# Router and gather on the raw residual sum, the first tile's routing inside the last projection, the expert's activation and down product bank by bank

## The chip, the core and the metric

The kernel runs on one core of one Trainium2 chip. It computes with TensorE (PE, matrix products; its weight loads are PEld), VectorE (DVE), ScalarE (ACT) and GpSimd (POOL); SyncE (SP) does little but issue DMA transfers, in the order of its queue, and an entry that waits holds back all behind it. The metric is the device time of one execution in microseconds (us). Runs of the kernel before lie between 2548.65 and 2553.27 us.

## The reference, cut to what matters

Two kinds of transformer blocks follow each other on 256 tokens of width 1024, all in float32. The change touches the end of the second: a mixer with three branches, gated, merged and projected (`w_out`), and then a mixture of 32 experts of which each token uses 4.

```python
h = rms_norm_2(x, norm_mix[layer]) * (1.0 + sc_m) + sh_m
branches = jnp.stack([o_lru, o_diff, o_swa], axis=2)
branch_proj = jnp.einsum('bsnc,ncd->bsnd', branches, w_branch)
gates = jax.nn.sigmoid(gl).reshape(B, S, N_BRANCHES, D)
merged = jnp.einsum('bsnd,bsnd->bsd', gates, branch_proj)
x = x + g_m * (merged @ w_out)
h = rms_norm_2(x, norm_ffn[layer]) * (1.0 + sc_f) + sh_f
logits = xt @ w_router + b_router            # xt = h
top_v, top_e = lax.top_k(logits, TOP_K)
hcat = x_pad[tok] @ w1[e] + b1[e]
x_glu = jnp.minimum(hcat[:, ::2], SWIGLU_LIMIT)
x_lin = jnp.clip(hcat[:, 1::2], -SWIGLU_LIMIT, SWIGLU_LIMIT)
act = x_glu * jax.nn.sigmoid(SWIGLU_ALPHA * x_glu) * (x_lin + 1.0)
return act @ w2[e] + b2[e]
```

## The kernel before, in words

Weights of the dense products come as 512 KB pieces into four rotating buffers named `raw` (`nraw` is 4); ACT rounds a piece to `whi`, DVE or POOL takes the rest into `wlo`, and PE multiplies three times (L205 to L207). A piece's buffer is free for the next load when both have read it. The kernel is written as a program whose instructions a scheduler puts in order on each engine; a buffer of a pool is handed out in program order, and an instruction that is "pinned" keeps its program order on its engine.

The end of the second block's mixer is written in this order: the sliding-window attention (`swa`, L1127 to L1185, called SWA here: scores L1158, bias L1165, softmax L438 to L453, products L1179 and L1182, and transposes, L233, at its end), then `prepare` (it opens the memory that SWA used as scratch for the experts, loads and prepares the router's constants in `route_prep`, and issues the first `npre` expert units), then `merge` (for each of three branches and two column halves 24 matmuls of a branch projection and 48 of its gate), then the last projection (`gemm` with `w_out`, eight pieces, the first tile of 128 tokens before the second). At the end of a tile its residual sum is formed (`done`), normalised and modulated (`rms_mod`, L872 and L873) and transposed; `route` computes logits, the choice and each token's place, and `moe_gather` collects the rows of a pair of experts by a one-hot product (L1369). The two vectors of the modulation occupy a buffer `AS` until then.

The experts (`moe`, L1535) go in 16 pairs; a pair's weights are 24 units of 1 MB (tiles `mraw`, one of the ring is `AS`), 16 for the up product (L1417) and 8 for the down product (L1456). SP issues all of them (L1482, the last in pieces at L1487) into a ring of 18 slots, each as soon as its slot is free. The first `npre` units go out in `prepare`, the others of the first 18 when the merge and the projection give memory back.

Of the kernel before, what the change touches and what calls it, by code (L numbers as in the profile page):

```python
# [18 lines left out]
P = 128  # L19
# [52 lines left out]
class Kernel:  # L72
    def __init__(self, tc, a, out, dbg=None):
# [7 lines left out]
        self.pre, self.npre = [], 4  # L81
# [32 lines left out]

    def small(self, n, tag="sm", dt=F32):
# [4 lines left out]
    def rsqrt(self, v, eps, n, scale=1.0):  # L120
# [6 lines left out]
        y = self.small(n, "ry")  # L127
# [723 lines left out]
    def rms_mod(self, t, h, A, sh, split=True):  # L851

# [9 lines left out]
        self.normed = nc.vector.tensor_tensor(ss[:, 2:3], ss[:, 0:1], ss[:, 1:2], op=OP.add)  # L862
        r = self.rsqrt(ss[:, 2:3], 1e-6, 1, 1.0 / D)
        xT = self.new_xT(t)
        def part(v, c):

            return v[:, c * 512:c * 512 + 512] if split else v.rearrange("t (p k) -> t k p", k=KD)[:, 4 * c:4 * c + 4]

        for c in range(2):
            s = slice(c * 512, c * 512 + 512)  # L870
            hv = h[:, s] if split else h[:, s].rearrange("t (k p) -> t k p", k=4)
            nc.vector.scalar_tensor_tensor(hv, part(x, c), r[:, 0:1], part(A, c), op0=OP.mult, op1=OP.mult)  # L872
            nc.vector.tensor_tensor(hv, hv, part(sh, c), op=OP.add)  # L873
# [317 lines left out]
    def hybrid_in(self, ctx, gp, first):  # L1191
# [3 lines left out]
        with tc.tile_pool(name="mix2", bufs=1, reuse_waits="tile") as mp:  # L1195
            gm = self.st(gp, [P, D], "gm")
            self.mod_row(gm, 2)
            A, sh = self.mod_pair(self.mods, 3, a["norm_ffn_2"][0])
# [39 lines left out]
            def prepare():  # L1238
# [5 lines left out]
                units(self.npre)  # L1244
# [518 lines left out]
```

## Time and profile before

| | |
|---|---|
| median of 3 runs | 2551.11 us (2548.65 to 2553.27) |
| the profiled execution | 2552.11 us, its span 2550.5 us (1.6 us lie outside the span) |
| PE busy | 2385.5 us, 94% |
| DVE, ACT, POOL busy | 50%, 32%, 9% |
| moved by DMA | 707.49 MB, 277 GB/s on average, 421 GB/s from some 1615 us to 2520 us |
| mean granted clock of TensorE | 0.977 of full speed |

Busy shares are averages over stages with different limits: PE counts as busy in the experts' stage too, where it mostly waits for the weights within a stream that the DMA engines run without a pause. What a stage is worth is read from the windows and from the chain of waits.

### The profile page before, as it was taken

To read this page: it belongs to the slowest core of one execution; us is meant where nothing else is said; L and a number is where in the kernel's file an instruction comes from. 1 tells how busy PE (TensorE), PEld (TensorE's weight loads), DVE (VectorE), ACT (ScalarE), POOL (GpSimd) and SP (SyncE) were. 2 spreads that over 40 slices of the span, in tenths; PEclk is the share of its full clock that TensorE was granted. 3 is DMA by queue.
4 is the path that set the end of the run, shared out by engine and by line. 5 is a ranking of instruction groups with operands and counts; after the bars stand their busy time and mean duration, and the time that the engine had idled before them with its cause. 6 is when DMAs were issued, how large, how long until landed. Compare 5 with 4: busy or idle time off the path is not lost.

```text
span 2550.5 us, 29146 instructions
## 1 busy us (share of the span) xinstructions
PE 2385.5 (94%) x11076; PEld 1571.2 (62%) x11076; DVE 1279.3 (50%) x2126; ACT 817.6 (32%) x1161; POOL 227.1 (9%) x200
## 2 busy tenths in 40 slices
PE   7998999999799999989988988999889998999998
PEld 6887787778678878878867766433333333333332
DVE  6768757576666675675566756222222222222222
ACT  5443544444344454444435653100000010000000
POOL 4000211200200011230022101000000000000000
PEclk9999999999899999999999999999999999999999
DMA  8777465577667656665646367899999999999997
GB/s 267 243 235 232 145 185 181 181 224 226 195 197 234 193 151 185 189 197 175 182 153 214 109 215 265 364 421 421 421 421 421 421 421 421 421 421 421 421 421 285
DMA packets 203145, 707.49 MB, mean 277 GB/s; under 512 B 18090, under 2 KB 31610, under 8 KB 154360
## 3 DMA queue, kind: packets, MB, share of 16 engines
q1 hardware_dynamic: 195368, 684.02, 73.7%
q0 software_dynamic: 7632, 21.55, 2.8%
q8 instruction: 89, 1.46, 0.2%
q14 instruction: 56, 0.46, 0.1%
HBM read 704.39 MB, written 3.47 MB: 278 GB/s over the span
## 4 chain that ended last, share of the span: by engine, by line
PE 40%; DMA 36%; DVE 7%; issue 2%; ACT 2%; POOL 1%; SPq 0%; DVEq 0%; ACTq 0%; POOLq 0%
DMA mraw<-in_w_dram 28%; PE mm L206 10%; PE mm L207 10%; PE mm L205 10%; DMA AS<-in_w_dram 3%; PE mm L1417 3%; PE tp L233 2%; DVE wlo L147 2%; DMA raw<-in_w_in_dram 1%; PE sc L1456 1%; DMA araw<-in_w_ada_dram 1%; ACT whi L143 1%; POOL wlo L147 1%; PE sc L1369 1%; DVE x L274 0%
## 5 line engine op out<-in xcount | busy, mean ns | idle before, releaser
L147 DVE TENSOR_TENSOR wlo<-raw,whi 128x1024 fp32r<-128x1024 f32 (+1 forms) x459 | 568.1, 1244 | 304.4 <-ACT whi L143 302.0
L143 ACT ACTIVATE whi<-raw 128x1024 fp32r<-128x1024 f32 x486 | 509.8, 1055 | 546.9 <-PE mm L207 385.5
L205 PE MATMUL mm<-whi,xTh 128*128 128x512 f32 (+2 forms) x1552 | 598.4, 387 | 9.1 <-ACT whi L143 9.1
L206 PE MATMUL mm<-wlo,xTh 128*128 128x512 f32 (+2 forms) x1552 | 593.0, 383 | 13.0 <-POOL wlo L147 8.9
L207 PE MATMUL mm<-whi,xTl 128*128 128x512 f32 (+2 forms) x1552 | 592.6, 382 | 0.4 <-DVE xTl L147 0.4
L1417 PE MATMUL mm<-mraw,xe 128*64 128x512 f32 x1968 | 495.4, 615 | 49.3 <-DMA mraw<-in_w_dram 49.3
L1417 PEld LDWEIGHTS mm<-mraw,xe 128*64 128x64 f32 x1968 | 156.3, 141 | 367.2 <-issue 265.5
L206 PEld LDWEIGHTS mm<-wlo,xTh 128*128 128x128 f32 x1552 | 294.9, 190 | 73.9 <-POOL wlo L147 11.9
L205 PEld LDWEIGHTS mm<-whi,xTh 128*128 128x128 f32 x1552 | 294.8, 190 | 66.2 <-ACT whi L143 11.7
L207 PEld LDWEIGHTS mm<-whi,xTl 128*128 128x128 f32 x1552 | 294.8, 190 | 52.0 <-DVE xTl L147 1.0
L1426 ACT ACTIVATE mt<-mg 128x256 f32<-128x256 f32 x64 | 26.7, 417 | 812.4 <-DVE mg L1425 762.4
L1425 DVE TENSOR_SCALAR mg<-mm 128x256 f32<-128x256 f32 x64 | 27.2, 425 | 462.1 <-PE mm L1417 457.7
L1456 PE MATMUL sc<-mraw,xTl 128*64 128x512 f32 x936 | 223.4, 594 | 0.2 <-ACT xTl L1440 0.2
L1456 PEld LDWEIGHTS sc<-mraw,xTl 128*64 128x64 f32 x936 | 71.5, 137 | 140.2 <-issue 136.7
L207 PE MATMUL mm<-whi,hl 128*128 128x512 f32 x352 | 138.3, 393 | 0.0
L205 PE MATMUL mm<-whi,hh 128*128 128x512 f32 x352 | 138.1, 392 | 0.0
L206 PE MATMUL mm<-wlo,hh 128*128 128x512 f32 x352 | 138.0, 392 | 0.0
L1461 DVE TENSOR_TENSOR xTh<-sc,gf 128x512 f32<-128x512 f32 x32 | 22.1, 692 | 215.7 <-PE sc L1456 215.7
L822 DVE SCALAR_TENSOR_TENSOR acc<-araw,cond,acc 128x512 f32<-128x512 f32 x96 | 71.8, 748 | 52.5 <-DMA araw<-in_w_ada_dram 51.9
L147 POOL TENSOR_TENSOR wlo<-raw,whi 128x1024 fp32r<-128x1024 f32 x27 | 69.0, 2569 | 281.3 <-ACT whi L143 277.7
L694 POOL TENSOR_TENSOR pj<-pj,gt 128x512 f32<-128x512 f32 x32 | 59.1, 1861 | 193.2 <-DVE gt L693 192.6
L206 PEld LDWEIGHTS mm<-wlo,hh 128*128 128x128 f32 x352 | 66.7, 189 | 13.7
(416 smaller groups left out, 2144.4 us busy)
## 6 DMA issues: line engine op xcount, KB each, us to landing
mraw<-in_w_dram SPq DMA_DIRECT2D x362, 1024.0 KB, 19.8
raw<-in_ffn_up_dram SPq DMA_DIRECT2D x176, 512.0 KB, 4.5
raw<-in_w_in_dram SPq DMA_DIRECT2D x142, 512.0 KB, 4.4
raw<-in_ffn_down_dram SPq DMA_DIRECT2D x88, 512.0 KB, 4.3
araw<-in_w_ada_dram SPq DMA_DIRECT2D x96, 256.0 KB, 4.1
AS<-in_w_dram SPq DMA_DIRECT2D x21, 1024.0 KB, 19.8
raw<-in_w_branch_dram SPq DMA_DIRECT2D x28, 512.0 KB, 3.7
raw<-in_w_out_dram SPq DMA_DIRECT2D x24, 512.0 KB, 4.4
```

What stands on the lines that cost most here:

```text
L143: ins = self.nc.scalar.activation(hi, src, AF.Copy)
L147: ins = (self.nc.gpsimd if pool else self.nc.vector).tensor_tensor(lo, src, hi, op=OP.subtract)
L205: nc.tensor.matmul(banks[b], xh, hi[:, s], start=kc == 0, stop=False)
L206: nc.tensor.matmul(banks[b], xh, lo[:, s], start=False, stop=False)
L207: nc.tensor.matmul(banks[b], xl, hi[:, s], start=False, stop=kc == nk - 1)
L233: self.nc.tensor.transpose(pt[:s.shape[-1], i * P:i * P + s.shape[0]], s, self.ident)
L694: nc.gpsimd.tensor_tensor(m, m, th, op=OP.add)
L822: nc.vector.scalar_tensor_tensor(acc, raw, self.cond[:, k:k + 1], acc, op0=OP.mult, op1=OP.add)
L1417: self.pe(nc.tensor.matmul(ph[nb][e * 64:e * 64 + 64], xe[:, k, e * 64:e * 64 + 64], units[e][k][:, nb * 512:nb * 512 + 512], start=False, ...
L1425: nc.vector.tensor_scalar(g, pv[:, :, 0], 7.0, None, op0=OP.min)
L1426: nc.scalar.activation(th, g, AF.Tanh, scale=0.851)
L1456: self.pe(nc.tensor.matmul(py[c][e * 64:e * 64 + 64], aT[:, k * P + e * 64:k * P + e * 64 + 64], w, start=k == 0, stop=k == 7))
```

## The change

The router and the gather work on the residual sum itself, not on its normalised and modulated copy. The scale per column (`acol`) goes into the router's matrix and, after the gather, into eight small operations per pair; the shift (`scol`) into the router's bias and the same eight; the token's norm (`rn`) multiplies logits and the one-hot matrix. So the two vectors of the modulation are loaded as columns, the buffer `AS` becomes the first slot of the ring (`npre` 5, the ring still has 18), and `route_prep` gains a product of router and shift, `prod`, which takes a buffer of the pool `raw`. The last projection is written out by hand (`out_and_route`, in an order that is kept), with the first tile's routing in it. Softmax and overflow count come behind the first up product (`route_rest`). A pair's activation, transposes and down product go bank by bank (`moe_body`). Every unit is a contiguous megabyte of W1 or W2 now, and the last two units come in halves of columns.

```diff
-        self.pre, self.npre = [], 4
+        self.pre, self.npre = [], 5
...
 
             self.st(mp, [33, 12], "rel")
...
+                units(self.npre - 1)
                 self.mi = 0
                 for src in self.sources(0)[:self.npre]:
...
+            grans = self.load_split(KD, a["w_out_2"][0], 0, D)
+            with self.ordered():
+                self.out_and_route(self.lhs_x(mT), grans, gm)
...
+    def out_and_route(self, lhs, grans, gm):
+
+
+
+
+        nc = self.nc
+        banks = self.banks(D)
+        for t in range(2):
+            self.products(lhs, KD, D, banks[t], t, grans[:1])
+        self.products(lhs, KD, D, banks[0], 0, grans[1:])
+        self.residual(0, 0, banks[0][0], gm)
+        self.residual(0, 1, banks[0][1], gm)
+        self.part(lhs, 1, banks[1][0], 0, grans[1:])
+        self.residual(1, 0, banks[1][0], gm)
+        self.turn(0, 0)
+        self.turn(0, 1)
+        self.part(lhs, 1, banks[1][1], 1, grans[1:4])
+        self.logits(0, 0)
+        self.logits(0, 1)
+        self.choose(0)
+        self.part(lhs, 1, banks[1][1], 1, grans[4:6])
+        self.place(0)
+        self.part(lhs, 1, banks[1][1], 1, grans[6:])
+        self.turn(1, 0)
+        self.gather_begin()
+        self.residual(1, 1, banks[1][1], gm)
+        self.logits(1, 0)
+        self.turn(1, 1)
+        self.logits(1, 1)
+        self.choose(1)
+        self.place(1)
...
+    def mod_cols(self):
...
+        def row(i):
+            return bass.AP(tensor=m.tensor, offset=m.offset + i * D, ap=[[1, P], [P, KD]])
+
+        self.acol, self.scol = col(row(4)), col(row(3))
+        norm = col(a["norm_ffn_2"][0].rearrange("(k p) -> p k", p=P))
+        nc.gpsimd.tensor_tensor(self.acol, self.acol, norm, op=OP.mult)
+        self.wr = self.cp.tile([P, KD, NE], F32, name="wr")
+        nc.gpsimd.dma_start(self.wr, a["w_router_2"][0].rearrange("(k p) n -> p k n", p=P))
...
+        prod = self.st(self.wp, [P, 1024], "raw", bufs=self.nraw)[:, :KD * NE]
+        v = prod.rearrange("p (n k) -> p k n", k=KD)
+        self.pin(nc.vector.tensor_tensor(v, self.wr, self.scol[:, :, None].to_broadcast([P, KD, NE]), op=OP.mult))
+        sw = self.st(mp, [P, NE], "lg0")
+        self.pin(nc.vector.tensor_reduce(sw, prod.rearrange("p (n k) -> p n k", k=KD), axis=AX.X, op=OP.add))
+        self.pin(nc.vector.tensor_tensor(self.wr, self.wr, self.acol[:, :, None].to_broadcast([P, KD, NE]), op=OP.mult))
+        pb = self.ps("tp")[:, :NE]
+        nc.tensor.matmul(pb, one, sw, start=True, stop=True)
+        self.pin(nc.vector.tensor_tensor(br, br, pb, op=OP.add))
...
+    def residual(self, t, h, bank, gm):
+
+        nc = self.nc
+        s = slice(h * 512, h * 512 + 512)
+        ss = self.sx[t]
+        y = self.st(self.fp, [P, 512], "y5", bufs=2)
+        nc.vector.scalar_tensor_tensor(y, bank, 0.5, gm[:, s], op0=OP.mult, op1=OP.mult)
+        nc.vector.tensor_tensor(self.h2[t][:, s], self.x[t][:, s], y, op=OP.add)
+        nc.scalar.activation(y, self.h2[t][:, s], AF.Square, accum_out=ss[:, h:h + 1])
+        if h == 0:
+            nc.vector.tensor_scalar(ss[:, 2:3], ss[:, 0:1], 1.0 / D, 1e-6, op0=OP.mult, op1=OP.add)
+        else:
+            self.rsqrt(ss[:, 1:2], ss[:, 2:3], 1, 1.0 / D, out=self.rn[:, t:t + 1])
+
...
+        lg = self.lg[t]
+        nc.vector.scalar_tensor_tensor(lg, self.pr[:, t * NE:t * NE + NE], self.rn[:, t:t + 1], self.rc[0], op0=OP.mult,
+                                       op1=OP.add)
...
+    def one_hot(self, S, t, pos, w):
+
+        for e in range(2):
+            f = w[:, t:t + 1] if len(w.shape) == 2 else w[:, t, e:e + 1]
+            self.nc.vector.tensor_scalar(S[:, t, e], self.slot, pos[:, t, e:e + 1], f, op0=OP.is_equal, op1=OP.mult)
...
+    def gather_end(self, mp, pg):
+
+        xe = self.st(mp, [P, KD, P], "xe")
+        for c in range(KD):
+            a, b = self.acol[:, c:c + 1], self.scol[:, c:c + 1]
+            src = pg[c // 4][:, c % 4 * P:c % 4 * P + P]
+            if c % 2:
+                self.nc.scalar.activation(xe[:, c], src, AF.Identity, scale=a, bias=b)
+            else:
+                self.nc.vector.tensor_scalar(xe[:, c], src, a, b, op0=OP.mult, op1=OP.add)
...
+    def moe_body(self, mp, ph, act, aT, ys, units, end=None):
+
+        py = [self.ps("sc") for _ in range(2)]
         for nb in range(4):
...
+            self.moe_act(mp, act, ph[nb], nb)
+        self.moe_aT(act, aT, 0)
+        for nb in range(1, 4):
+            self.moe_aT(act, aT, nb)
+            self.moe_down(py, aT, units, nb - 1)
+        if end:
+            end(None)
+        for c in range(2):
+            if end or c == 0:
+                self.moe_down(py, aT, units, 3, (c,) if end else (0, 1), bool(end))
+            self.moe_scale(ys, py, c)
+            if end:
+                end(c)
...
+        def of(w, d):
+            return w[e + d] if isinstance(e, int) else w[bass.ds(e[d], 1)].rearrange("o f n -> (o f) n")
+
+        up = [of(W1, d).rearrange("(k p) n -> p k n", p=P)[:, k] for k in range(KD) for d in range(2)]
+        return up + [of(W2, d).rearrange("(j p r) n -> p j (r n)", p=P, r=2)[:, j] for j in range(4) for d in range(2)]
...
-        ph, xe = self.ph0, self.moe_gather(mp, self.pos[:, :, 0:2])
+        u1, u2 = self.moe_load(0)
+        with self.ordered():
+            self.one_hot(self.S0, 1, self.pos[:, :, 0:2], self.rn)
+            self.gather_tile(self.pg0, self.S0, 1)
+            xe = self.gather_end(mp, self.pg0)
+            ph = self.moe_bias(self.sel, self.b1[0])
+            self.moe_up(xe, ph, u1)
+            self.route_rest(self.bp)
+            for t in range(2):
+                nc.scalar.activation(self.x[t], self.h2[t], AF.Copy)
...
+                self.moe_up(xe, ph, u1)
+            if not end:
+                xe = self.moe_gather(mp, self.pos[:, :, e + 2:e + 4])
+                nxt = self.moe_load(e + 2)
```

On **SP** the program's order around the end of SWA was, before, as follows (`raw` from `w_branch` and `w_in` are pieces for the merge, `mraw` are expert units; 16 pieces for the merge stand ahead of the units, of which the last four are shown):

```order
L219 DMA raw_12746<-in_w_branch_dram 128x2x512
L219 DMA raw_12752<-in_w_branch_dram 128x2x512
L219 DMA raw_12788<-in_w_in_dram 128x2x512
L219 DMA raw_12794<-in_w_in_dram 128x2x512
L1482 DMA mraw_12502<-in_w_2_dram 128x2048
L1482 DMA mraw_12504<-in_w_2_dram 128x2048
L1482 DMA mraw_12506<-in_w_2_dram 128x2048
L1482 DMA mraw_12508<-in_w_2_dram 128x2048
L219 DMA raw_12800<-in_w_in_dram 128x2x512
L219 DMA raw_12806<-in_w_in_dram 128x2x512
```

After the change the same queue reads as follows, from the last two pieces of the gates that stand before SWA's end in both on:

```order
L237 DMA raw_12397<-in_w_in_dram 128x2x512
L237 DMA raw_12403<-in_w_in_dram 128x2x512
L1612 DMA mraw_12528<-in_w_2_dram 128x2048
L1612 DMA mraw_12530<-in_w_2_dram 128x2048
L1612 DMA mraw_12532<-in_w_2_dram 128x2048
L1612 DMA mraw_12534<-in_w_2_dram 128x2048
L237 DMA raw_12536<-in_w_branch_dram 128x2x512
L237 DMA raw_12542<-in_w_branch_dram 128x2x512
L237 DMA raw_12576<-in_w_in_dram 128x2x512
L237 DMA raw_12582<-in_w_in_dram 128x2x512
```

The four units, which wait for SWA's memory, stand ahead of all 28 pieces that the merge still needs; before, they stood ahead of 12 of them.

On **PE** the merge's matmuls (`mm` from `whi` or `wlo`) stood between SWA's before; this is a stretch of them near SWA's end (`tp` with `ident` are transposes, `sc` SWA's products):

```order
L206 MATMUL mm_12693<-wlo_12683,xTh_2403_11114 128x512
L233 MATMUL tp_12275<-ident,s_2650_12236 128x128 x2
L207 MATMUL mm_12693<-whi_12682,xTl_2404_11115 128x512
L205 MATMUL mm_12692<-whi_12688,xTh_2381_10996 128x512
L233 MATMUL tp_12275<-ident,s_2650_12236 128x128 x2
L206 MATMUL mm_12692<-wlo_12689,xTh_2381_10996 128x512
L1179 MATMUL sc_12263<-pj_11990,s_2660_12269 128x64 x4
L233 MATMUL tp_12287<-ident,s_2623_12121 128x128 x4
L207 MATMUL mm_12692<-whi_12688,xTl_2382_10997 128x512
L205 MATMUL mm_12692<-whi_12688,xTh_2381_10996 128x512
L1179 MATMUL sc_12263<-pj_11990,s_2662_12280 128x64 x4
```

After the change SWA's own stand alone, and the first of the branch product follows the last of SWA and the new router product (L1361):

```order
L1184 MATMUL sc_12266<-pj_11993,s_2661_12272 128x64 x4
L251 MATMUL tp_12290<-ident,s_2624_12124 128x128
L1184 MATMUL sc_12266<-pj_11993,s_2663_12283 128x64 x4
L251 MATMUL tp_12290<-ident,s_2624_12124 128x128 x3
L251 MATMUL tp_12297<-ident,s_2624_12124 128x128 x4
L1361 MATMUL tp_12494<-lg_2709_12491,one_12487 128x32
L223 MATMUL mm_12548<-whi_12538,yT1h_2418_11161 128x512
L223 MATMUL mm_12549<-whi_12538,yT1h_2420_11163 128x512
```

Counted over the stretch, 141 of these matmuls stood ahead of SWA's last transposes, and none does now: all 336 (six halves of branch products with 24 each, four halves of gates with 48) follow.

On **DVE**, after the change, SWA's last rows are followed by the preparation of the router, and the first `wlo` of the merge comes some rows behind it:

```order
L471 RECIPROCAL rs_2658_12264<-se_2656_12255 128x4
L1187 TENSOR_TENSOR s_2624_12124<-sc_12266,rs_2658_12264 128x256
L1349 MEMSET tri_12484 128x128
L165 TENSOR_TENSOR yT2l_2423_11166<-tp_12290,yT2h_2422_11165 128x512
L165 TENSOR_TENSOR yT2l_2425_11168<-tp_12297,yT2h_2424_11167 128x512
L1344 TENSOR_TENSOR b_2702_12471<-raw_12470,b_2702_12471 64x512
L1344 TENSOR_TENSOR b_2704_12477<-raw_12476,b_2704_12477 64x512
L1347 TENSOR_TENSOR pick_12482<-ident 128x64
L1353 MEMSET one_12487 128x128
L1356 TENSOR_TENSOR raw_12489<-wr,mc_11147 128x8x32
L1367 MEMSET on_12499 128x32
L1528 CAST sel_12512<-pick_12482 128x512
```

Before, SWA's last group (from one L1182 to the scores' maximum L438 and on) stood on DVE with the pieces' `wlo` between:

```order
L1182 TENSOR_TENSOR s_2623_12121<-sc_12212,rs_2644_12210 128x256
L147 TENSOR_TENSOR wlo_12683<-raw_12680,whi_12682 128x1024
L1165 SCALAR_TENSOR_TENSOR s_2650_12236<-sc_12237,ry_2615_12084,s_2607_12065 128x256
L1165 SCALAR_TENSOR_TENSOR s_2650_12236<-sc_12238,ry_2615_12084,s_2607_12065 128x256
L1165 SCALAR_TENSOR_TENSOR s_2650_12236<-sc_12237,ry_2615_12084,s_2607_12065 128x256
L1165 SCALAR_TENSOR_TENSOR s_2650_12236<-sc_12238,ry_2615_12084,s_2607_12065 128x256
L147 TENSOR_TENSOR wlo_12689<-raw_12686,whi_12688 128x1024
L438 TENSOR_REDUCE mx_2653_12247<-s_2650_12236 128x4
L440 TENSOR_TENSOR mx_2653_12247<-mx_2653_12247,sk_2603_12055 128x4
L442 TENSOR_SCALAR nb_2654_12250<-mx_2653_12247 128x4
```

In the rows of after no `wlo` stands before SWA's end; `raw` at L1356 is `prod`, and the pieces of the merge that come later in the program get their `raw` buffers behind it.

At the end of the last projection PE's order is now this, from the projection's last matmul to the first up product (`tp` with `h` transposes, `sc` from `S` and `h` is the gather, `mm` from `wr` the logits):

```order
L1308 MATMUL mm_13200<-whi_13193,xTl_2849_13099 128x512
L251 MATMUL tp_13362<-ident,h_13145 128x128 x4
L1480 MATMUL sc_13368<-S_2906_13370,h_13144 128x128 x4
L1480 MATMUL sc_13369<-S_2906_13370,h_13144 128x128 x4
L1406 MATMUL mm_13327<-wr,xTh_2901_13360 128x32 x4
L251 MATMUL tp_13403<-ident,h_13145 128x128 x4
L1406 MATMUL mm_13327<-wr,xTh_2901_13360 128x32 x4
L1430 MATMUL mm_13327<-mask_12504,tri_12484 128x32
L1432 MATMUL mm_13327<-mask_12504,one_12487 128x32
L1480 MATMUL sc_13368<-S_2906_13370,h_13145 128x128 x4
L1480 MATMUL sc_13369<-S_2906_13370,h_13145 128x128 x4
L1535 MATMUL mm_13518<-b_2702_12471,sel_12512 128x512
```

Of the gather of the first pair the first tile's half stands ahead of the second tile's choice, and no operation on `h` as a whole stands between the residual sum and the transposes.

## Rows read from the trace of the kernel before

**Rows 1.** The page: bytes in 40 equal slices, the chain by line, one DMA line.

```profile
GB/s 267 243 235 232 145 185 181 181 224 226 195 197 234 193 151 185 189 197 175 182 153 214 109 215 265 364 421 421 421 421 421 421 421 421 421 421 421 421 421 285
...
DMA mraw<-in_w_dram 28%; PE mm L206 10%; PE mm L207 10%; PE mm L205 10%; DMA AS<-in_w_dram 3%; PE mm L1417 3%; PE tp L233 2%; DVE wlo L147 2%; DMA raw<-in_w_in_dram 1%; PE sc L1456 1%; DMA araw<-in_w_ada_dram 1%; ACT whi L143 1%; POOL wlo L147 1%; PE sc L1369 1%; DVE x L274 0%
...
raw<-in_w_in_dram SPq DMA_DIRECT2D x142, 512.0 KB, 4.4
```

**Rows 2.** Windows by stage (from:to, length, busy time by engine, clock, DMA share, GB/s).

```profile
1457.40:1504.00 46.60, 44.42 (x243) 35.31 (x243) 32.24 (x67) 25.89 (x59) 1.19 (x3) 1.00 0.47 142
...
1522.00:1557.40 35.40, 34.78 (x143) 27.86 (x144) 26.40 (x23) 20.28 (x22) 7.05 (x4) 0.94 0.80 264
...
1586.20:1609.30 23.10, 15.37 (x89) 14.27 (x87) 12.35 (x58) 3.16 (x7) 0.73 (x2) 0.70 0.82 324
...
1606.00:1613.00 7.00, 7.00 (x40) 4.48 (x40) 0.49 (x2) 1.19 (x2) 0.00 (x0) 0.86 0.00 1
...
1700.00:2300.00 600.00, 557.24 (x2514) 214.50 (x2511) 131.68 (x282) 42.24 (x90) 0.00 (x0) 0.98 1.01 421
```

**Rows 3.** Timeline around SWA's end: SP, ACT and PE (start, length, operation, idle before).

```profile
1503.97 3.06 SPq L1482 DMA_DIRECT2D mraw<-in_w_dram  x4
...
1521.47 1.06 ACT L143 ACTIVATE whi<-raw 128x1024 fp32r<-128x1024 f32 x1 [14.49 <-DMA raw<-in_w_in_dram]
...
1513.67 0.39 PE L206 MATMUL mm<-wlo,xTh 128*128 128x512 f32 x1
...
1515.25 0.39 PE L207 MATMUL mm<-whi,xTl 128*128 128x512 f32 x1
1522.58 1.22 PE L205 MATMUL mm<-whi,xTh 128*128 128x512 f32 x2 [6.94 <-ACT whi L143]
```

**Rows 4.** DVE by line, 1457.4 to 1504 us.

```profile
L147 DVE TENSOR_TENSOR wlo<-raw,whi 128x1024 fp32r<-128x1024 f32 x13 | 15.9, 1221 | 3.1 <-ACT whi L143 3.1
```

**Rows 5.** Timeline: one group of SWA on DVE and ACT.

```profile
1477.93 0.69 DVE L1182 TENSOR_TENSOR s<-sc,rs 128x512 f32<-128x512 f32 x1 [2.31 <-PE sc L1179]
...
1479.67 1.65 DVE L1165 SCALAR_TENSOR_TENSOR s<-sc,ry,s 128x256 f32<-128x256 f32 x4
...
1482.51 1.21 DVE L438 TENSOR_REDUCE mx<-s 128x4 f32<-128x1024 f32 x1
...
1485.63 0.51 ACT L445 ACTIVATE s<-s,nb 128x256 f32<-128x256 f32 x1 [1.05 <-DVE nb L442]
...
1487.71 1.27 ACT L1175 ACTIVATE s<-tp 128x512 f32<-128x512 f32 x2
...
1490.38 0.42 DVE L1182 TENSOR_TENSOR s<-sc,rs 128x256 f32<-128x256 f32 x1 [2.16 <-PE sc L1179]
```

**Rows 6.** Windows: a stretch with PE idle for most of it, and the next.

```profile
1320.00:1330.00 10.00, 4.17 (x14) 1.84 (x13) 8.79 (x24) 5.21 (x10) 1.50 (x3) 0.73 0.45 137
1330.00:1335.00 5.00, 5.00 (x13) 3.94 (x13) 1.23 (x2) 0.58 (x2) 2.90 (x2) 0.51 0.97 334
```

**Rows 7.** Timeline from the last projection to the first up product.

```profile
1581.45 0.63 PE L233 MATMUL tp<-ident,h 128*128 128x128 f32 x4 [1.71 <-DVE h L873]
...
1586.15 3.01 SPq L1482 DMA_DIRECT2D mraw<-in_w_dram  x6
...
1591.32 2.18 DVE L872 SCALAR_TENSOR_TENSOR h<-x,ry,AS 128x512 f32<-128x512 f32 x2
...
1595.53 0.33 SPq L1482 DMA_DIRECT2D AS<-in_w_dram  x1
...
1603.31 6.02 PE L1369 MATMUL sc<-S,h 128*128 128x128 f32 x32
...
1609.26 7.09 PE L1417 MATMUL mm<-mraw,xe 128*64 128x512 f32 x32
...
1612.94 0.80 SPq L1482 DMA_DIRECT2D mraw<-in_w_dram  x2
```

**Rows 8.** Timeline of PE, the last pair.

```profile
2526.24 0.64 PE L1456 MATMUL sc<-mraw,xTl 128*64 128x512 f32 x1 [0.25 <-ACT xTl L1440]
```

More of the change, by code (lines that the diff above doesn't have):

```diff
@@ L113, in pin, with ordered @@
         self.tc.keep_in_program_order(ins)
+    @contextmanager
+    def ordered(self):
+        cur = self.nc.cur_bb
+        traced = cur.bb.instructions
+        last = traced[-1]
+        yield
+        assert self.nc.cur_bb is cur
+        start = next(k for k in reversed(range(len(traced))) if traced[k] is last) + 1
+        chain = mybir.DependencyInfo(mybir.DependencyClass.NoSync, mybir.DependencyReason.DATA)
+        for engine in (mybir.EngineType.PE, mybir.EngineType.DVE, mybir.EngineType.Activation):
+            prev = next((i for i in reversed(traced[:start]) if i.engine == engine), None)
+            for i in traced[start:]:
+                if i.engine == engine:
+                    if prev is not None:
+                        self.tc.add_manual_dep(i, prev.name, chain, reason="ordered")
+                    prev = i
     def small(self, n, tag="sm", dt=F32):
@@ L1305, in route, with gather_begin, route_rest @@
+    def gather_begin(self):
+        self.pg0 = [self.ps("sc") for _ in range(2)]
+        self.S0 = self.st(self.bp, [P, 2, 2, CAP], "S0")
+        self.one_hot(self.S0, 0, self.pos[:, :, 0:2], self.rn)
+        self.gather_tile(self.pg0, self.S0, 0)
+    def route_rest(self, mp):
+        nc = self.nc
+        br, tri, one, on = self.rc
+        mask = self.mask
         cnt = self.st(mp, [P, NE], "cnt")
+        pc = self.ps("tp")[:, :NE]
+        for u in range(2):
+            nc.tensor.matmul(pc, one, mask[:, u], start=u == 0, stop=u == 1)
+        nc.vector.tensor_copy(cnt, pc)
@@ L1405, in moe_bias, with moe_up @@
         return ph
[L1407 removed]
+    def moe_up(self, xe, ph, units):
         nc = self.nc
@@ new lines, in moe_aT, with moe_down @@
+    def moe_aT(self, act, aT, nb):
+        pt = self.ps("tp")
+        for r in range(2):
+            self.pe(self.nc.tensor.transpose(pt[:, r * P:r * P + P], act[:, nb, r], self.ident))
+        self.nc.scalar.activation(aT[:, nb * 256:nb * 256 + 256], pt[:, :256], AF.Copy)
+    def moe_down(self, py, aT, units, j, cs=(0, 1), last=False):
+        for r in range(2):
+            for c in cs:
+                o = c * D + r * 512 if last else r * D + c * 512
+                for e in range(2):
+                    k = (2 * j + r) * P + e * 64
+                    self.pe(self.nc.tensor.matmul(py[c][e * 64:e * 64 + 64], aT[:, k:k + 64], units[e][j][:, o:o + 512],
+                                                  start=j == 0 and r == 0, stop=j == 3 and r == 1))
```

302 lines of the change are left out of this document (130 added, 172 removed).

## The prediction

> **What bounds the kernel now.** The chain of waits first: its largest entry is PE waiting for expert weights, and in the slices from about 1615 us on the DMA engines move a flat 421 GB/s [rows 1]. The windows say the same: from 1700 to 2300 us the DMA share is 1.01 [rows 2]. A unit is 1.0486 MB, so 2.49 us each, and nothing that PE does in that stage changes its length. What can change the time is when this stream starts to run without a pause, its rate, and what follows its last byte. So I read backwards from its start. Between 1606 and 1613 us it stands still (1 GB/s [rows 2]): all 18 slots are full, and SP waits until the first up product frees one; it issues again at 1612.94 [rows 7], with 366 of 384 units still to come. Before that lie the last projection with the routing, and before it the merge, where PE is the limit (143 matmuls in 34.78 of 35.40 us, [rows 2]), and SWA, which PE bridges with the merge's matmuls: 44.42 us busy of 46.60 [rows 2], although SWA alone leaves it mostly idle.
>
> **SWA and merge.** On PE 141 merge matmuls stood under SWA and none does now; on DVE the 13 `wlo` of that stretch, 15.9 us [rows 4], leave as well. The reason is in the buffers: two of the four `raw` are held by the experts' biases until SWA ends, `prod` now takes the third, and the fourth is queued on SP behind units that wait for SWA's memory.
>
> SWA becomes shorter. One group ran from the L1182 at 1477.93 to the next at 1490.38, 12.45 us [rows 5]. Alone it needs: bias 1.65, maximum 1.21, small steps 0.4, four exponentials 2.1 (1485.63 to 1487.71), transposes copied 1.27, the product's rest behind the copy 1.4 (to 1490.38), 0.42: 8.4 us. So each of the two later groups saves about 4, the first about 3.5 (its wait for the last `sc` remains), and the start comes 3 earlier, without the two `wlo` (1.22 each, [rows 4]) and two gated products that stood in the chain ahead of it: SWA would end 14.7 before the 1503.97 at which the units were issued [rows 3], at 1489.3. That is with PE at full clock, as in the row of this stage (1.00). But now PE is nearly idle in it; earlier, in a stretch with 4.17 us busy of 10, the row shows 0.73, and 0.51 in the next [rows 6]. PE's share of the chain, about 4.7 us of products that something waits for, then doubles: 1494. The Trainium skill (TensorE: Matmul & The Clock Gate, "HAM oscillation — how this bites in real kernels") has the array fall to its slower clock in such waits; by it 1494, by the stage's own row 1489.3, and I take 1494, bounds 1489 and 1498.
>
> Then PE has nothing. Before, the first piece issued behind the four units reached ACT at 1521.47, 17.5 us after the units' issue; ACT had waited 14.49 and PE 6.94 [rows 3], since 49 matmuls covered the rest. That cover is gone. The bound below is 4.72 MB at 421 GB/s and a landing of 2.4 (derived below), 13.6 us; above, 17.5. Fewer pieces share the queue now; I take 16, and 1.1 for `whi` [rows 3]: PE starts 17.1 after SWA, at 1511.1. All 336 matmuls follow at 0.226 each (seven in 1513.67 to 1515.25, [rows 3]), 76 us; the stretch before lost 3.0 beside that (35.40 less 143 times 0.2265), mostly at the slow clock after the gap, so 78.5. The merge ends at 1589.6 instead of 1557.4: **+32 us**, bounds +23 and +42.
>
> **Projection and routing.** The gemm itself loses a stall for the first tile's `h` (1.71 and its neighbours, 2.7 in all, [rows 7]) and gains logits and place, about 2.2: no change; it ends 28.8 us after the merge, as at 1586.15, when SP issues the last units of the ring [rows 7]. Seven units came then (six, and `AS` at 1595.53, held by the modulation), drained by 1606: 17.4 us of bytes and 2.4 of landing. Now six come: filled after 14.9 + 2.4 = 17.3 us. The first up product began 23.1 us after the gemm's end [rows 2]. It now loses L872 and L873 (2.18 and as much again, 4.2), three quarters of the gather, 4.5 of 6.02 [rows 7], and about 4 of transposes and logits that run beside the norm instead of behind it; it gains 0.6 in eight small ends: 11 us. SP gets a slot 3.7 after that start (1609.26 to 1612.94), and its bytes flow 2.4 later, at 17.1, just ahead of 17.3: the stream no longer pauses. It resumed at 1612.94 + 2.4 = 29.2 us after the gemm's end; now it runs on at 17.3. **Gain 11.9**; with 3 us less, 9. More is not to be had however fast the routing is, because the ring's last six units are issued at the gemm's end in both.
>
> **The rest.** Stream: 366 units in both, no change. Tail: DMA has drained before the last down product starts to run out; PE is the limit there, with the same products; the waits ahead of 2526.24 (0.25 in its row [rows 8], about 1.5 with its neighbours) go, since the down product of a bank no longer waits for all four: −1.5, bounds −4 and +1. Columns instead of rows for the modulation, and a unit of 1 MB on SP early in the mixer where 1.5 MB on POOL's queue stood: both beside PE's work of the diff projections, 0, bounds ±3. Softmax and counting behind the first up product lie under the stream. Eight small operations per pair instead of two lie there too: DVE and ACT have 78% and 93% idle in it [rows 2].
>
> **The sum.** 2552.1 (the profiled execution, 1.0 above the median) + 32.2 − 11.9 − 1.5 = 2570.9; against the median, **2570 us**. The bounds together would give 2551 + (23 − 15 − 4) to 2551 + (42 − 9 + 1), that is 2555 to 2585.
>
> **Rivals.**
> - *The contiguous units run faster.* W1's partitions lay 64 KB apart, and are adjacent now. It needs 430 GB/s instead of 421 to take back the 19.2 us (911.3 × 9/430), and above that the change is faster. Against it: the slices are flat at 421 with the DMA share at 1.01 [rows 1, 2], over W1 and W2 units, whose partitions lay differently far apart, alike. At 3% more it would be 2543. The Trainium skill (DMA: Bandwidth & Descriptors, "Latency and other measured facts") says that rows at large power-of-two distances slow copies and contiguous tiles restore them; by its "Where 436 GB/s comes from" the ports end at 435, an estimate of 882 us for the stream and 2541 for the whole. No row here shows more than 421 over a slice. Chance 0.07.
> - *The merge's gap is short.* If the first piece lands in its usual 4.4 us [rows 1], interleaved with the units, and SWA keeps the full clock, the merge ends at 1489.3 + 5.5 + 78.5 = 1573.3, +16 instead of +32; with −13.4 it is 2554, within 0.2%. Against: the 14.49 us that ACT waited [rows 3]. Chance 0.08.
> - *The pieces starve the merge longer.* Three pieces wait for DVE's rows of preparation, and four buffers refill one by one beside units: 10 to 20 us more, 2580 to 2590. Chance 0.15.
> - My forecast, 0.70.
>
> 0.2% is 5 us, about what a measurement of this kernel tells from no change. Faster 0.08, same 0.09, slower 0.83. The range takes in the bounds and most of the starved case: 2554 to 2588.
>
> **What would show it.** Right: in the windows, PE busy far below a half for some 30 us before the units' issue; ACT idle some 15 us behind it with the release by DMA; 336 matmuls behind that; no window at 1 GB/s between the projection and the first up product; 421 GB/s again. Wrong: `mm` rows of the merge among SWA's, units issued later than 1500, a stream above 425, or a pause in front of it.

## The result and the profile after

The changed kernel took 2582.97 us (median of 4 runs, 2581.60 to 2588.15) beside 2552.03 us for the kernel before (4 runs): a ratio of 1.0127, 95% interval 1.011 to 1.0145, or 31 us more. The profiled execution took 2583.36 us, its span 2581.8 us, 31.3 more than that of before.

The page of the changed kernel: PE's share of the span by slice of 64.5 us, what the DMA engines moved by slice, and the chain of work that ended last.

```profile
PE   8998999999799999999988769999999999999998
...
GB/s 270 236 240 227 146 194 181 177 230 240 169 215 226 200 137 189 185 190 187 196 177 150 21 236 228 331 420 421 420 420 421 420 421 421 421 421 421 421 420 290
...
DMA mraw<-in_w_dram 20%; PE mm L224 12%; PE mm L225 12%; PE mm L223 12%; PE mm L1548 7%; PE sc L1579 5%; PE tp L251 3%; DMA araw<-in_w_ada_dram 2%; DVE wlo L165 2%; PE tp L1654 1%; DMA raw<-in_ffn_up_dram 1%; ACT whi L161 1%; PE sc L1480 1%
```

The plateau of 420 to 421 GB/s is the one of [rows 1], at the same height. New is the slice with 21 GB/s, from about 1420 to 1484 us. That is where SWA stands, so the windows are cut around it, in the columns of [rows 2] (busy time and count of each engine, granted clock, DMA share, GB/s): SWA; the gap behind it; the merge; the last projection; from the gemm's end to the first up product; the start of the stream; the stream.

```profile
1448.60:1497.60 49.00, 31.57 (x118) 22.59 (x116) 19.20 (x60) 12.95 (x46) 1.10 (x3) 0.54 0.00 1
1497.60:1515.20 17.60, 0.61 (x3) 0.51 (x3) 4.33 (x13) 2.58 (x4) 0.45 (x2) 0.50 0.97 359
1515.20:1595.30 80.10, 80.06 (x338) 64.84 (x339) 48.77 (x45) 39.24 (x42) 10.59 (x6) 0.97 0.69 217
1595.30:1626.00 30.70, 28.55 (x138) 23.30 (x137) 14.14 (x37) 7.52 (x14) 3.48 (x2) 0.94 0.60 240
1626.00:1640.00 14.00, 11.18 (x68) 9.81 (x66) 7.00 (x30) 3.29 (x7) 0.54 (x1) 0.76 0.92 357
1641.00:1646.00 5.00, 5.00 (x26) 1.59 (x24) 0.00 (x0) 2.62 (x5) 0.00 (x0) 1.00 0.71 259
1700.00:2300.00 600.00, 569.32 (x2551) 212.66 (x2550) 149.87 (x350) 48.31 (x130) 0.00 (x0) 0.97 1.01 421
```

In the stretch of SWA the instructions on PE fell from 243 [rows 2] to 118: the merge's matmuls that had stood between SWA's, called the bridge from here on, are gone. The granted clock fell from 1.00 to 0.54 (1.00 is the upper of its two levels, 2.4 GHz, and 0.50 the lower, 1.2 GHz), and DMA from 142 GB/s to 1. Then PE had three instructions in 17.6 us. The whole merge stands behind that: 80.1 us of PE at its limit, 338 instructions.

What PE and SP waited for there is in the queue's own waits (engine, what it waited for, total us, times, longest) and in the timeline of SP, DVE, ACT and PE (start, length, operation, idle before and its releaser):

```profile
SPq L1612 <- DVE s L1187: 82.9, 1, 82.9
```

```profile
1454.40 1.08 PE L251 MATMUL tp<-ident,s 128*128 128x128 f32 x4 [5.43 <-DVE s L1142]
...
1471.01 0.69 DVE L1187 TENSOR_TENSOR s<-sc,rs 128x512 f32<-128x512 f32 x1 [5.15 <-PE sc L1184]
...
1477.15 2.16 PE L251 MATMUL tp<-ident,s 128*128 128x128 f32 x8 [3.32 <-ACT s L463]
1479.20 1.97 PE L1184 MATMUL sc<-pj,s 128*128 128x64 f32 x8
...
1482.25 1.97 PE L1184 MATMUL sc<-pj,s 128*128 128x64 f32 x8
1484.15 2.66 PE L1163 MATMUL sc<-s,s 64*128 64x256 f32 x6
1484.25 0.42 DVE L1187 TENSOR_TENSOR s<-sc,rs 128x256 f32<-128x256 f32 x1 [5.18 <-PE sc L1184]
1490.12 2.17 PE L251 MATMUL tp<-ident,s 128*128 128x128 f32 x8 [3.32 <-ACT s L463]
...
1495.99 0.42 DVE L1187 TENSOR_TENSOR s<-sc,rs 128x256 f32<-128x256 f32 x1 [3.95 <-PE sc L1184]
...
1497.59 2.08 SPq L1612 DMA_DIRECT2D mraw<-in_w_dram  x4
1499.78 1.58 SPq L237 DMA_DIRECT2D raw<-in_w_branch_dram  x2
...
1514.08 1.06 ACT L161 ACTIVATE whi<-raw 128x1024 fp32r<-128x1024 f32 x1 [14.96 <-DMA raw<-in_w_branch_dram]
...
1595.08 0.60 PE L251 MATMUL tp<-ident,pj 128*128 128x128 f32 x4
...
1626.10 0.60 PE L251 MATMUL tp<-ident,h 128*128 128x128 f32 x4
1634.59 3.78 PE L1480 MATMUL sc<-S,h 128*128 128x128 f32 x16 [0.85 <-DVE S L1476]
1638.03 2.00 PE L1535 MATMUL mm<-b,sel 128*128 128x512 f32 x4
1639.96 0.64 PE L1548 MATMUL mm<-AS,xe 128*64 128x512 f32 x1
...
1643.64 0.33 SPq L1612 DMA_DIRECT2D AS<-in_w_dram  x1
...
2551.50 3.65 PE L1579 MATMUL sc<-mraw,xTl 128*64 128x512 f32 x16 [1.32 <-ACT xTl L1570]
```

SP stood for 82.9 us at a unit whose memory SWA held, and the first piece of the merge is the entry behind the four units that this wait held. ACT idled 14.96 us for it, as it had idled 14.49 in [rows 3], but now PE had nothing meanwhile.

Cut at the merge's end (before 1557.4 [rows 2], after 1595.1) and at SP's next unit after the ring is full (1612.94 [rows 7] and 1643.64), the 31.3 us come out as: **+37.7** up to the merge's end, **−7.0** from there to SP's resumption (55.5 to 48.5), **+0.6** from there to the end of the span (937.6 to 938.2). The two cuts at the merge's end are not quite the same event: 1557.4 is the end of the window in [rows 2], which the forecast uses too, and 1595.1 the first of the transposes behind the merge, which stand here in the kernel before:

```profile
1557.68 0.60 PE L233 MATMUL tp<-ident,pj 128*128 128x128 f32 x4
```

By the transposes in both it is 37.4 us more up to the merge's end and 6.7 less from there to SP's resumption.

### The profile page after: what moved, and what is told of

Its sections match the earlier page's. It is cut to its first block, busy times and chain, and to the rows that moved or that the text cites. A ratio compares the mean times of both kernels' runs of the same rounds, so it can differ in the third digit from the quotient of the medians.

```text
span 2581.8 us, 29399 instructions
## 1 busy us (share of the span) xinstructions
PE 2408.3 (93%) x11078; PEld 1576.8 (61%) x11078; DVE 1305.4 (51%) x2234; ACT 830.7 (32%) x1227; POOL 227.8 (9%) x200
## 4 chain that ended last, share of the span: by engine, by line
PE 57%; DMA 27%; DVE 9%; issue 3%; ACT 3%; POOL 1%; SPq 0%; DVEq 0%; ACTq 0%; POOLq 0%
DMA mraw<-in_w_dram 20%; PE mm L224 12%; PE mm L225 12%; PE mm L223 12%; PE mm L1548 7%; PE sc L1579 5%; PE tp L251 3%; DMA araw<-in_w_ada_dram 2%; DVE wlo L165 2%; PE tp L1654 1%; DMA raw<-in_ffn_up_dram 1%; ACT whi L161 1%; PE sc L1480 1%; DMA raw<-in_w_in_dram 1%; DVE acc L840 1%
## 5 line engine op out<-in xcount | busy, mean ns | idle before, releaser
L224 PE MATMUL mm<-wlo,xTh 128*128 128x512 f32 (+2 forms) x1538 | 586.8, 382 | 10.4 <-POOL wlo L165 7.8
L225 PE MATMUL mm<-whi,xTl 128*128 128x512 f32 (+2 forms) x1538 | 586.7, 382 | 0.4 <-DVE xTl L165 0.4
L1548 PE MATMUL mm<-mraw,xe 128*64 128x512 f32 x1920 | 487.1, 611 | 40.3 <-DMA mraw<-in_w_dram 40.3
L1579 PE MATMUL sc<-mraw,xTl 128*64 128x512 f32 x976 | 231.0, 598 | 8.8 <-ACT xe L1491 7.4
```

What stands on the lines that cost most here:

```text
L224: nc.tensor.matmul(banks[b], xh, lo[:, s], start=False, stop=False)
L225: nc.tensor.matmul(banks[b], xl, hi[:, s], start=False, stop=kc == nk - 1)
L1548: self.pe(nc.tensor.matmul(ph[nb][e * 64:e * 64 + 64], xe[:, k, e * 64:e * 64 + 64], units[e][k][:, nb * 512:nb * 512 + 512], start=False, ...
L1579: self.pe(self.nc.tensor.matmul(py[c][e * 64:e * 64 + 64], aT[:, k:k + 64], units[e][j][:, o:o + 512], start=j == 0 and r == 0, stop=j == ...
```

## The experiments

Times are medians, each beside runs of the kernel before on the same chip. "Base" is the kernel that the edit starts from. The theory was that `prod`'s buffer keeps the merge's matmuls from standing under SWA; the rivals were that the order of the units on SP does, that the number of `raw` buffers does, and, for the gain, that it lies elsewhere in the routing.

**e1_own: `prod` in a tile of its own memory.** Base: the changed kernel.

```diff
-        prod = self.st(self.wp, [P, 1024], "raw", bufs=self.nraw)[:, :KD * NE]
+        prod = self.st(mp, [P, 2, 2, CAP], "S0").rearrange("p t e s -> p (t e s)")
```

> The changed kernel, but prod lies in a tile of its own memory (that of S0, unused until later) instead of a raw buffer. Theory (prod keeps the merge's pieces from getting buffers until SWA has ended): 141 merge matmuls stand under SWA again, the merge ends near 1554 us, the expert stream resumes 48 us later as in the changed kernel, and the time is 2542 us (2537 to 2549), below both kernels. Rival (the preparation pinned on DVE or the routing itself costs it): the merge still ends after 1580 and the time stays above 2565.

Measured: 2545.22 us (10 runs), ratio 0.9971, interval 0.9961 to 0.9981. Windows of this kernel: SWA, the rest of the merge, the start of the stream; and SWA's second group of products on PE.

```profile
1455.00:1501.90 46.90, 44.63 (x237) 35.34 (x236) 31.13 (x65) 25.70 (x59) 1.09 (x2) 0.96 0.45 136
1501.90:1556.80 54.90, 48.31 (x197) 38.20 (x196) 32.24 (x38) 23.83 (x27) 10.00 (x8) 0.91 0.84 283
...
1603.00:1608.00 5.00, 5.00 (x26) 1.72 (x24) 0.00 (x0) 2.31 (x5) 0.00 (x0) 1.00 0.74 265
```

```profile
1486.21 1.89 PE L1184 MATMUL sc<-pj,s 128*128 128x64 f32 x16
```

One tile's place gave the bridge back: 237 instructions of PE under SWA (243 before, 118 in the changed kernel), clock 0.96, and a merge that ends at 1556.8. From there SP's resumption comes 48.5 us later, as in the changed kernel, against 55.5 before. So the 38 us are the bridge, all of them, and the rest of the change is worth some 7 us in this run (4 in its repetition, e10_pair below). This kernel is faster than both others.

**e2_hold: the reverse, one held buffer in the kernel before.** It adds one instruction and leaves the routing as it was.

```diff
+        hold = self.st(self.wp, [P, 1024], "raw", bufs=self.nraw)[:, :KD * NE]
+        self.pin(nc.vector.memset(hold, 0.0))
```

> The kernel before with one addition: a raw buffer that nothing reads is taken in route_prep and first written by a pinned memset of 0.2 us. Theory: this alone brings the loss, all 336 merge matmuls behind SWA, the merge's end 40 us later and 2590 us (2582 to 2598), more than the changed kernel, since the gain in the routing is missing. Rival (the loss needs the new routing, columns or ring): within 5 us of before, 2552.

Measured: 2591.86 us (4 runs), ratio 1.015, interval 1.0134 to 1.0167: +39 us. Its windows over SWA and the gap, and ACT's first piece in its timeline:

```profile
1457.40:1501.80 44.40, 31.20 (x116) 22.61 (x116) 14.87 (x44) 12.11 (x44) 1.05 (x2) 0.50 0.00 1
1501.84:1517.00 15.16, 0.00 (x0) 0.00 (x0) 3.27 (x8) 1.53 (x3) 0.83 (x3) 0.50 0.95 338
```

```profile
1519.14 1.06 ACT L143 ACTIVATE whi<-raw 128x1024 fp32r<-128x1024 f32 x1 [15.77 <-DMA raw<-in_w_branch_dram]
```

The same picture without any of the new routing: a buffer that is taken for one pinned instruction is sufficient.

**e3_raw5: five buffers instead of four.** Base: the changed kernel.

```diff
-        self.nraw, self.nhl, self.next, self.xp = 4, 7, 4, None
+        self.nraw, self.nhl, self.next, self.xp = 5, 7, 4, None
```

> The changed kernel with five raw buffers instead of four, so that two stay free for the merge's pieces as before. If the count of free buffers is what is missing, as the prediction has it: 2542 us (2537 to 2549). If a buffer of the pool can't be handed on past prod, which asks for its own before the pieces do and is written only when SWA has ended: as the changed kernel, 2583 us (2576 to 2590).

Measured: 2576.99 us (4 runs), ratio 1.0096, interval 1.0079 to 1.0113. The window of SWA:

```profile
1442.90:1491.90 49.00, 31.60 (x118) 22.60 (x116) 19.19 (x60) 12.94 (x46) 1.53 (x4) 0.54 0.03 11
```

A fifth buffer brings back not one matmul (118, as before the edit), so the number of buffers isn't what shuts the bridge off. The median lies 6 us below that of the changed kernel. In the profiled executions the merge ends 8.6 us earlier (1586.4): 5.7 of these lie ahead, since SWA begins and ends that much earlier at the same length, and 3.0 between SWA's end and the merge's (94.5 us for 97.5). Why SWA began earlier was not traced; between two executions of one kernel below, e8_outside and e11_pair, its begin differs by 3.1 us.

**e5_early: the same buffer, first written before SWA.** Base: the changed kernel. A write that is not pinned goes ahead of the pinned product, so the buffer is handed out early; it is then held as long as before.

```diff
         prod = self.st(self.wp, [P, 1024], "raw", bufs=self.nraw)[:, :KD * NE]
+        nc.gpsimd.memset(prod, 0.0)
```

> The changed kernel, prod in its raw buffer, but first written by a memset on POOL that waits for nothing in SWA. Three of four buffers are held all the same, one is left. If the count is the cause: as the changed kernel, 2583 us (2576 to 2590). If the order in which the pool hands out is: 84 matmuls of the merge return under SWA, about 57 (13 us) and some of the gap of 17 us stay behind it, and the time is 2560 us (2550 to 2570).

Measured: 2560.24 us (10 runs), ratio 1.0033, interval 1.0023 to 1.0042. The first write of the buffer, and windows of SWA, of the gap, and of SWA again, from the transposes ahead of its first scores to the units' issue:

```profile
1422.66 0.31 POOL L1355 MEMSET raw<- 128x256 f32 x1 [1.59 <-DVE wlo L165]
```

```profile
1450.00:1494.80 44.80, 38.76 (x198) 27.63 (x196) 26.64 (x66) 20.99 (x54) 0.52 (x1) 0.96 0.24 72
1494.80:1512.00 17.20, 3.34 (x14) 2.10 (x12) 6.36 (x16) 2.33 (x4) 1.35 (x4) 0.75 0.95 360
...
1457.00:1494.84 37.84, 33.68 (x178) 24.36 (x178) 19.99 (x44) 19.49 (x52) 0.56 (x2) 0.95 0.24 70
```

The last stretch once more, in the changed kernel:

```profile
1454.40:1497.59 43.19, 31.19 (x116) 22.56 (x116) 13.87 (x39) 12.15 (x44) 1.09 (x2) 0.50 0.00 1
```

With three of the four buffers held all through SWA, and only one left to rotate, some 80 of the 336 merge matmuls stand under SWA again (198 instructions instead of 118, in a window of 44.8 us), the clock is 0.96, and the merge ends at 1569.9, 25 us earlier than in the changed kernel. So what blocked was the turn: buffers are handed out in program order, `prod` is due before the merge's next pieces, its first write is pinned behind SWA on DVE, and every later request for a `raw` waits for it. Having one buffer less is worth the rest: 13 us between this kernel's merge end and that of e1_own. The two windows of SWA as a whole show one thing more. With the clock kept and 6 `wlo` of DVE in it, where e1_own has 12, SWA took 37.8 us here; it took 43.2 in the changed kernel without any `wlo` but at 0.50, and 43.8 in e1_own.

**e4_late: the expert units written behind the merge.** Base: the changed kernel; it tests whether the pieces wait for the buffer or for the units that stand ahead of them on SP.

```diff
-                for src in self.sources(0)[:self.npre]:
-                    self.pre.append(self.unit(src))
...
             mg = self.merge(mp, lhs, w, 3328, a["w_branch_2"][0], yTs, (1, 0, 2), 4, prepare)
+            for src in self.sources(0)[:self.npre]:
+                self.pre.append(self.unit(src))
```

> The changed kernel with the first five expert units written behind the merge in the program: SP's queue has one unit instead of four ahead of the merge's pieces. SWA still stands alone on PE. Theory (the 16.5 us from SWA's end to the first piece are the four units' transfer): the first piece lands some 7 us after SWA's end, the merge ends 9 us earlier and the time is 2573 us (2568 to 2578). Rival (DVE's preparation and the pool set that wait): 2583 us.

Measured: 2579.57 us (4 runs), ratio 1.0103, interval 1.0089 to 1.0118: between the two expectations. The timeline of SP and ACT:

```profile
1502.11 0.34 SPq L1612 DMA_DIRECT2D mraw<-in_w_dram  x1
1502.50 1.94 SPq L237 DMA_DIRECT2D raw<-in_w_branch_dram  x2
...
1517.35 0.42 SPq L1612 DMA_DIRECT2D mraw<-in_w_dram  x1
...
1510.58 1.06 ACT L161 ACTIVATE whi<-raw 128x1024 fp32r<-128x1024 f32 x1 [6.94 <-DMA raw<-in_w_branch_dram]
```

Only one unit is now ahead of the pieces, and ACT gets the first 8.5 us after it (16.5 in the changed kernel). From the first unit's issue to the merge's end it took 88.8 us instead of 97.5. But in this execution SWA began 4.5 us later, and from the merge's end on it took 988.3 us instead of 986.7; the median shows 3.4 us, and the ratios to the kernel before on each chip, 1.0103 and 1.0127, some 6. The gap's length comes from the units ahead of the first piece; that there is a gap does not: the pieces still don't come before SWA's end.

**e7_bias: the expert's bias product ahead of the second tile's gather.** Base of this and of the next ones: e1_own. It asks whether the gain of the routing is held by the first up product or by the ring's last six units.

```diff
+            ph = self.moe_bias(self.sel, self.b1[0])
             self.one_hot(self.S0, 1, self.pos[:, :, 0:2], self.rn)
             self.gather_tile(self.pg0, self.S0, 1)
             xe = self.gather_end(mp, self.pg0)
-            ph = self.moe_bias(self.sel, self.b1[0])
```

> The kernel with prod in its own tile (first experiment), and the four bias products of the first pair put ahead of the second tile's gather, into PE's wait for the choice. If the start of the first up product holds the stream's resumption: 2.0 us earlier, 2543 us against 2545, the pause before the stream shorter by as much. If the ring's last units, issued at the gemm's end, hold it: no change, 2545.

Measured: 2547.67 us (11 runs), ratio 0.9976, interval 0.9968 to 0.9985. The windows around the first up product, which begins at 1606.1:

```profile
1604.00:1609.00 5.00, 5.00 (x30) 2.99 (x31) 1.91 (x5) 2.33 (x7) 0.00 (x0) 0.93 1.02 424
1609.00:1614.00 5.00, 5.00 (x26) 1.72 (x24) 0.00 (x0) 1.71 (x2) 0.00 (x0) 1.00 1.01 419
```

And the 100 us from the merge's end on, of e1_own and of e7_bias:

```profile
1556.80:1656.80 100.00, 93.35 (x455) 54.49 (x454) 37.62 (x121) 19.18 (x40) 4.02 (x3) 0.93 0.86 348
```

```profile
1563.40:1663.40 100.00, 94.17 (x463) 53.81 (x463) 40.25 (x125) 18.86 (x40) 4.02 (x3) 0.96 0.87 355
```

SP resumed 46.3 us after the merge's end instead of 48.5, and the small pause (265 GB/s in e1_own, 259 in the changed kernel) was gone: 424 and 419. So the first up product no longer holds the stream, which is 0.7 MB ahead after 100 us (355 GB/s against 348), about 1.7 us at 421 GB/s. Little of that reached the end: from the merge's end to the end of the span it took 986.2 us against 986.8, one execution each. The medians can't decide between 2 us and nothing, since the ratio lies between those of e1_own and e10_pair (0.9971 and 0.9985), which are one and the same kernel. Where the rest of the 1.7 us went was not traced.

**e9_body: all four transposes before the first down product**, as the pair was ordered before; the activation stays bank by bank.

```diff
-        self.moe_aT(act, aT, 0)
-        for nb in range(1, 4):
+        for nb in range(4):
             self.moe_aT(act, aT, nb)
+        for nb in range(1, 4):
             self.moe_down(py, aT, units, nb - 1)
```

> The kernel with prod in its own tile, but all four banks of a pair transposed before the first down product, as before the change. If the stream hides a pair's order, and only the last pair shows it: 2545 to 2547 us, stream rate 421 GB/s, the tail behind the last unit up to 2 us longer. If the bank by bank body feeds the stream by freeing slots earlier: 2550 or more.

Measured: 2546.11 us (9 runs), ratio 0.9981, interval 0.9971 to 0.9991; 985.5 us from the merge's end on. That part of the change is worth nothing that shows.

**e8_outside, e10_pair and e11_pair: the first tile's routing behind the projection again.** e10_pair is e1_own once more and e11_pair is e8_outside once more, side by side on one chip, since the first e8_outside agreed with neither expectation.

```diff
+        self.part(lhs, 1, banks[1][1], 1, grans[1:])
         self.turn(0, 0)
         self.turn(0, 1)
-        self.part(lhs, 1, banks[1][1], 1, grans[1:4])
         self.logits(0, 0)
         self.logits(0, 1)
         self.choose(0)
-        self.part(lhs, 1, banks[1][1], 1, grans[4:6])
         self.place(0)
-        self.part(lhs, 1, banks[1][1], 1, grans[6:])
```

> The kernel with prod in its own tile, with the first tile's transposes, logits, choice and place behind the last projection instead of inside it. The gemm ends some 4 us earlier, and with it the issue of the ring's last six units; the first up product stands some 2 to 4 us later after the merge's end, since the first tile's chain is no longer covered. If that start holds the stream: 2548 us (2546 to 2550). If the ring's last units hold it: 2542 us.

> The same kernel as e1_own, once more, beside e11_pair on one chip: 2545 us (2542 to 2548) by every theory.

> The same kernel as e8_outside, beside e10_pair on one chip. Theory that what precedes the merge only wanders from execution to execution and the order of the first tile's routing costs only what shows from the merge's end on: 1.3 us above e10_pair (988.1 against 986.8 us from the merge's end in the two profiles), so 2545 to 2548. Rival, that routing inside the projection is itself worth what the first two medians differ by: 5 to 6 us above e10_pair, 2550 to 2552.

Measured: e8_outside 2551.54 us (12 runs), ratio 0.9991, interval 0.9979 to 1.0003. e10_pair 2548.40 us (12 runs), 0.9985, 0.9977 to 0.9994; e11_pair 2553.19 us (12 runs), 0.9999, 0.9991 to 1.0008. So the order inside the projection is worth 4.8 us on this chip, against the theory that e11_pair's expectation puts first, and it is nearly all that the change gains: without it the kernel stands at 0.9999 and 0.9991 of before. The window between the projection's last matmul and the first up product, of e10_pair, e11_pair and e8_outside in turn:

```profile
1589.30:1603.10 13.80, 10.97 (x65) 9.64 (x63) 7.00 (x30) 3.29 (x7) 0.54 (x1) 0.76 0.95 364
```

```profile
1586.50:1608.10 21.60, 16.86 (x93) 15.11 (x91) 8.87 (x41) 4.33 (x9) 0.54 (x1) 0.68 0.79 311
```

```profile
1587.80:1606.00 18.20, 13.45 (x93) 11.95 (x91) 8.87 (x41) 4.29 (x9) 0.54 (x1) 0.91 0.93 369
```

From the merge's end to SP's resumption it was 48.6 us in e10_pair, 53.0 in e11_pair and 48.2 in e8_outside, which is the same kernel as e11_pair. The difference between these two executions goes with the clock: 3.4 us of it lie in this block of 93 instructions in both, at 0.68 against 0.91 (16 gather products take 2.92 us in the one and 2.05 in the other), and 1.5 in the projection ahead of it, at 0.94 against 1.00. So routing as one block of small products behind the projection can keep its clock, and then costs nothing up to SP's resumption. How often it does was not traced beyond these two profiles. The runs give a hint: 4 of the 24 runs of that order lie under 2548.5 us, and 15 of the 22 of the interleaved one; those 4 have a mean granted clock of 0.978 or 0.979, the other 20 of 0.973 to 0.977. That mean covers the whole execution, though, and the one profile that kept the clock in the block belongs to a run of 2551.14 us. There the time went elsewhere: the merge ended at 1561.5 us, 4.6 later than in e1_own.

## Why the prediction was right

Forecast +19 us against the median, measured +31; the sign and the chain of events held, and the time lies inside the range, near the upper end of its bounds (2585). That is in part luck: the terms missed by 5.5, 4.8 and 2.1 us, all the same way, and within the first of them two larger errors offset each other. By its own steps:

- **SWA stands alone, the pieces come behind the units, the whole merge follows.** Right: 118 instructions on PE, 14.96 us of ACT's wait released by DMA, 338 instructions in one piece. **+37.7** instead of +32.2. Of the 5.5 us, 3.6 are SWA's end (1497.6 for 1494), 0.5 the gap (17.6 for 17.1) and 1.4 the matmuls (79.9 for 78.5, from 1515.2 to 1595.1).
- **The step that was mis-sized is "SWA becomes shorter".** A group alone was put at 8.4 us at full clock, with "about 4.7 us of products" that would double, once for all of SWA. Cut at the division L1182 (L1187 now) as there, the two later groups took 13.24 and 11.74 us (1471.01, 1484.25, 1495.99), together no less than the 12.45 [rows 5] and 11.93 (to 1502.31) with the bridge; all of SWA, from the transposes ahead of its first scores to the units' issue, took 43.2 us instead of 42.1. The clock stands at 0.50 over all of that and is paid in every group: eight L1184 took 1.97 us where 16 had taken 1.89 in e1_own, and of the 12.97 us from one group's transposes to the next's, 9.7 pass from the first transposes to the end of the next scores (1477.15 to 1486.81), PE's share of the chain with its short waits for ACT. What the missing `wlo` gave, the clock took. e5_early shows the two apart: at 0.95 and with half of the `wlo` gone SWA took 37.8 us. That SWA ended 6.4 us earlier than before [rows 3] comes from its begin alone: the transposes ahead of its first scores stand at 1454.40 instead of 1461.92. The forecast had that begin 3 us earlier, and 3.3 is what the held buffer alone gave (1458.65 in e2_hold). The other 4 are not explained, and they hid part of the error in the groups.
- **The cause that was given for it was half wrong.** That two of the four `raw` are held, that `prod` takes the third and that the fourth is queued on SP behind units counts buffers. e3_raw5 refutes the count, and e5_early, with three held, restores some 80 of the matmuls of the bridge and 25 of the 38 us. It is the order of hand-out, a request whose first use is late, that shuts the pool; the units on SP only lengthen the gap (e4_late). The forecast's +32 didn't depend on which, but a repair would have: one more buffer would have been the wrong one.
- **Routing −11.9**: measured −7.0, mis-sized too. The gemm, called unchanged at 28.8 us, took 31.0 (1595.1 to 1626.1), and the first up product came 13.9 us behind it, not 11: the second half of the gather and the bias product run in a clock of 0.52 from 1635 to 1640 us (3.78 us for 16 products that took 1.95 in the first half). SP resumed 17.5 us after the gemm, so with 2.4 us of landing the bytes flow at 19.9, not at 17.1, which is 2.6 behind the 17.3 at which the ring is filled, and a small pause is left (259 GB/s). The 2.2 of the gemm and these 2.6 are the 4.8 above.
- **"More is not to be had however fast the routing is"**: open. With the pause gone and SP 2.2 us earlier, e7_bias has its stream 1.7 us ahead, so an earlier start was to be had there; its end came 0.6 us sooner, and its median shows no gain.
- **Tail −1.5**: measured +0.6 with all that follows the resumption. The wait ahead of the last pair's down product did not go; it now reads 1.32 us for ACT's transposed copy, where [rows 8] has 0.25.
- **The rivals.** Contiguous units: 421 GB/s before and after, [rows 2]; the Trainium skill (DMA: Bandwidth & Descriptors, "Latency and other measured facts") warns of rows at large power-of-two distances, from 512 KiB up, and the trace shows no gain from removing a shorter one of 64 KB. The short gap: 17.6 us, refuted. Starving pieces: the merge ran at 80.06 of 80.10 us, refuted; 2583 lies in that rival's range (2580 to 2590) for other reasons, the three terms above.

The Trainium skill (TensorE: Matmul & The Clock Gate, "HAM oscillation — how this bites in real kernels") lets an array with waits between short bursts fall to its slower clock. The trace agrees, 0.54 over 49 us, though its waits are for ACT and DVE; the forecast charged the slower clock with 4.7 us in all, and it cost more.

## What to carry to other kernels

A tile from a rotating pool that is first written by an instruction that must wait closes the pool to every later request; the price is the work that those requests would have fed, here 38 us for a 1 KB-per-row scratch tile, and not the buffer itself. When a long chain of small steps is bridged by other work, look under it after every change in memory or order, since the bridge carries the matrix engine's clock as well as its own work. A faster stage ahead of a saturated stream is worth what reaches the end: in e7_bias the stream ran 1.7 us ahead and the end came 0.6 us sooner, so look for the next limit before counting the rest.

## What the runs showed of the hardware that was not expected

SWA alone was hardly faster than SWA with the merge's matmuls in between: from the transposes ahead of its first scores to the units' issue 43.2 us in the changed kernel (1454.40 to 1497.59) and 43.8 in e1_own (1458.10 to 1501.90), at clocks of 0.50 and 0.96. With half of the bridge it was the shortest, 37.8 us at 0.95 (e5_early). And one and the same order of small products (e8_outside and e11_pair) was granted 0.91 in one execution and 0.68 in another, 18.2 and 21.6 us for the same 93 instructions, where the order interleaved with dense matmuls showed 0.76 in both of its windows here (14.00 us in the changed kernel, 13.80 in e10_pair).
